# Output projection of an encoder layer: the matmuls that sum the squares a tick and a half later, residual adds on another engine, another order of free banks

## The chip, the cores and the metric

One core of a Trainium2 chip runs the whole program. The metric is device time in microseconds, the median of several runs. The engines are TensorE (PE for matmuls, PEld for its weight loads), VectorE (DVE), ScalarE (ACT), GpSimd (POOL) and SyncE (SP, which here issues DMAs in the order of its queue). Each engine works through its own list of instructions in order, and waits at an instruction until what it needs is there.

## What is computed

A bidirectional encoder layer on two requests (256 and 1024 tokens, width 1024): a half-step SwiGLU network, a mixture of two kinds of attention, a projection of their joint output, a second SwiGLU network, a final norm. The part that matters here, with `oa` and `ob` the two attention outputs, 512 wide each:

```
def rmsnorm(x, g):
    return x * rsqrt(mean(x * x) + EPS) * g
...
mix = concat([rmsnorm(oa, out_norm_a), rmsnorm(ob, out_norm_b)]) @ w_out   # 1024 x 1024
x = x + rmsnorm(mix, mix_post)
x = x + 0.5 * rmsnorm(swiglu(rmsnorm(x, ffn2_pre), ffn2_w_gu, ffn2_w_down), ffn2_post)
```

Everything is fp32; a matmul splits each operand into a high and a low fp32r part and adds three products.

## The kernel before

The class `MixOut` is the output projection. The 1280 tokens are cut into five pieces of 256 and each piece into its two halves of 512 inputs (A and B): ten *operands*, n = 0 to 9, in the order `seq`. An operand has two row tiles of 128 tokens, and each tile two halves of 512 outputs; so `product(n, i, s)` runs four times per operand, each time a group of 12 matmuls (four blocks of inputs, three products) into one bank of PSUM, `yps`. The norms' factors are applied behind the matmul, since they belong to a token. A piece's A half is evacuated by ACT (L1115) into a tile y; its B half is added onto y by DVE (L1124).

`operands` prepares an operand in three stages (the `yield`s part them):

1. SP loads it (`ml`, L1072).
2. ACT makes the high part `mh` (L1077, four instructions) and squares all of it into `sq` (L1078); POOL folds the four blocks of `sq` into one (L1080, two adds); DVE makes the low part in place (L1082, four). There is one buffer `sq`, and L1082 overwrites what L1078 reads.
3. PE sums the squares over the inputs with a matmul against ones (`ssq`, L1088, two of 128x1); DVE adds EPS (L1090); POOL takes the power −1/2 (L1091): the factor `ro`, which the evacuations need.

`done` finishes a tile: SP loads the residual x1 (L1121) and DVE evacuates; ACT squares y (L154) and POOL works out its factor `rs` (L162, L163); DVE multiplies (L1128); POOL adds onto the residual (L1130); SP stores it (L1132); ACT, POOL and DVE do the same for the next norm (L154, L162, L163, L148); SP stores the result (L1136, `xnd`). The second network fetches it again (L1451), POOL forms differences of it (L204 to L216 in `GateUp.blocks`), PE transposes (L197, `tr`), ACT and DVE split (L199, L200).

What sets the order: a pipe (`Pipe`). It counts ticks, one per tile of an operand; a work item comes with a plan of (lag in ticks, place within the tick, cost) for each stage. Stages of a tick run in the order of the place, and the four product groups of the two ticks are laid between them. From the program so written a scheduler makes each engine's list by its own estimate of times, so a moved stage shifts others too. PREP is the plan of `operands`, DONE that of `done`:

```
PREP = [(0, 0, 0.0), (1, 2, 0.0), (3, 0, 0.0)]
DONE = [(0, 1, 0.0), (0, 3, 0.0), (1, 4, 0.0), (2, 2.5, 0.0), (2, 6, 0.0), (3, 6, 0.0), (3, 6, 0.0)]
```

PSUM banks are given out in turn from lists (`Banks.use`): the projection has banks 2 to 5 for products and 6, 7, 0, 1 for transposes and sums of squares; the second network's gate and up products have 0 to 3, and its first transposes take 4 to 7. The last two groups of the projection stand in banks 4 and 5.

Of the kernel before, what the change touches and what calls it, by code (L numbers as in the profile page):

```python
# [13 lines left out]
ALU = mybir.AluOpType  # L14
# [128 lines left out]
def normed(c, x, gain, junk):  # L143

    nc = c.nc
    r = row_factor(c, [square(c, x, junk)])
    yield
    nc.vector.scalar_tensor_tensor(x, x, r, gain, op0=ALU.mult, op1=ALU.mult)  # L148


def square(c, x, junk):

    ss = c.small.tile([128, 1], F32, name="ss")
    c.nc.scalar.activation(junk[:, :x.shape[1]], x, AF.Square, scale=1 / 32, accum_out=ss)  # L154
    return ss


def row_factor(c, sums):

    nc = c.nc  # L160
    r = c.small.tile([128, 1], F32, name="rs")
    nc.gpsimd.tensor_scalar(r, sums[0], sums[1] if len(sums) == 2 else 0.0, EPS, op0=ALU.add, op1=ALU.add)  # L162
    nc.gpsimd.tensor_tensor(r, r, c.mhalf, op=ALU.pow)  # L163
    return r


class GateUp:
# [64 lines left out]
    def prep(self, f):  # L232

        c, nc = self.c, self.c.nc
        g, u = self.raw.pop(f)
        g0, g1, u0, u1 = g[:, 0:4], g[:, 4:8], u[:, 0:4], u[:, 4:8]
        A = self.A[f] = [None] * 7

        def put(i, src):
            A[i] = [self.wp.tile([128, 4, 128], F32R, name=n, bufs=8) for n in ("ah", "al")]  # L240
            split(c, A[i][0], A[i][1], src)

        def tmp(name):
            return self.wp.tile([128, 4, 128], F32, name=name, tag="s", bufs=2)

        put(0, g0)
        yield
        s1, s2 = tmp("s1"), tmp("s2")
        nc.vector.tensor_tensor(s1, u0, u1, op=ALU.add)
        nc.vector.tensor_tensor(s2, s1, g0, op=ALU.subtract)  # L250
        put(1, s2)
        yield
        put(2, g1)
        nc.vector.tensor_tensor(s2, g1, s2, op=ALU.subtract)
        put(4, s1)
        yield
        s3 = tmp("s3")
        nc.vector.tensor_tensor(s3, g0, u0, op=ALU.subtract)
        put(3, s3)
        yield  # L260
        put(5, u1)
        yield
        put(6, s2)
        yield
# [734 lines left out]
class MixOut:  # L999
# [55 lines left out]

    def prep(self, n):
        if n < len(self.seq):
            self.c.pipe.start(self.operands(*self.seq[n], n not in (3, 6)), self.PREP)

    def operands(self, t, half, own):  # L1060

# [47 lines left out]
    def done(self, t, half, i, pss):  # L1109
        c, nc = self.c, self.c.nc  # L1110
        r = self.r[t, half][:, i:i + 1]
        if half == 0:
            y = self.y[t + i] = self.a.tile([128, D], F32, name="y", bufs=4)
            for s, ps in enumerate(pss):
                nc.scalar.activation(y[:, s * 512:(s + 1) * 512], ps, AF.Copy, scale=r)  # L1115
            return
        t += i
        y = self.y.pop(t)
        k = self.k
        x1 = k.tile([128, D], F32, name="x1", bufs=3)  # L1120
        nc.sync.dma_start(x1, self.x1d[t])  # L1121
        for s, ps in enumerate(pss):
            o = y[:, s * 512:(s + 1) * 512]
            nc.vector.scalar_tensor_tensor(o, ps, r, o, op0=ALU.mult, op1=ALU.add)  # L1124
        yield
        junk = k.tile([128, D], BF16, name="junk")
        r = row_factor(c, [square(c, y, junk)])
        nc.vector.scalar_tensor_tensor(y, y, r, self.gmp, op0=ALU.mult, op1=ALU.mult)  # L1128
        yield
        nc.gpsimd.tensor_tensor(x1, x1, y, op=ALU.add)  # L1130
        yield
        nc.sync.dma_start(self.x2d[t], x1)  # L1132
        junk = k.tile([128, D], BF16, name="junk")
        yield from normed(c, x1, self.gf2, junk)
        yield
        nc.sync.dma_start(self.xnd[t], x1)  # L1136
# [25 lines left out]
def encoder(tc, i, out_p, out_s):  # L1162
    nc = tc.nc
    c = Ctx()
# [37 lines left out]
    GATE = {f"{n}{b}": (4 * i + b,) for i, n in enumerate("AB") for b in range(4)}  # L1202
# [275 lines left out]
    mo.close()  # L1478
    gu.open_chunk(1, L.open("xbB", 1))
    gu.work = L.open("gw2", 2)  # L1480
    c.ps.use(**dict(GATE, tr=(4, 5, 6, 7)))
    first = gu.steps(0)
    rest = (None for p in range(2, 5) for _ in gu.blocks(p, *fetch2(p)))
    for step in first[:7]:
# [63 lines left out]
def build(nc, arrays):  # L1548
    ins = {}
    for name, a in arrays.items():  # L1550
        ins[name] = nc.dram_tensor(f"in_{name}_dram", a.shape, mybir.dt.from_np(a.dtype), kind="ExternalInput").ap()
    outs = [nc.dram_tensor(f"out_{i}_dram", s, F32, kind="ExternalOutput").ap()
            for i, s in enumerate(((1, 256, 1024), (1, 1024, 1024)))]
    with tile.TileContext(nc) as tc:  # L1554
        encoder(tc, ins, *outs)
# [12 lines left out]
```

## Time and profile before

| | us |
|---|---|
| median of three runs | 2361.4 (2359.25, 2361.4, 2364.24) |
| profiled execution, whole | 2363.55 |
| its span, first to last instruction | 2361.8 |
| granted TensorE clock, mean | 0.979 |
| output projection, its part behind the attention | about 1376 to 1507 in the span |
| second network behind it | about 1507 to the end |

In the profile's rows, a line number names a line of the kernel, `out<-in` the tiles, `xcount` how many instructions stand in a row, and a bracket at the end how long the engine was idle before it and what released it. A row of a timeline starts with its start and its duration in us. A row of a table of groups has, behind the bar, the busy time in us and the mean in ns of one, and then the idle time ahead of them.

### The profile page before, as it was taken

How to read it: one execution, taken by the hardware profiler on the slowest of the kernel's cores; microseconds unless marked ns; L12 is line 12 of the kernel's file. 1: busy time of each engine (PE TensorE's matmuls, PEld its weight loads, DVE VectorE, ACT ScalarE, POOL GpSimd, SP SyncE). 2: the span in 40 equal slices, each digit the busy share in tenths (PEclk: the TensorE clock that was granted, in tenths of full speed). 3: DMA queues.
4: the chain of work that ended last, by engine and by line, in shares of the span. 5: the costliest groups of instructions: out<-in, count | busy, mean ns of one | idle time of the engine just before them, and what ended most of it. 6: DMA issues, size and time to landing. Idle time of an engine off the chain costs nothing. (4 is left out here: it accounts for less than half of the span.)

```text
span 2361.8 us, 37120 instructions
## 1 busy us (share of the span) xinstructions
PE 2247.5 (95%) x13208; PEld 2047.1 (87%) x13208; DVE 1464.3 (62%) x2575; ACT 980.7 (42%) x2043; POOL 726.7 (31%) x835
## 2 busy tenths in 40 slices
PE   6999999999999999999999788799999999999997
PEld 5999999999788788888888667699999999988876
DVE  7666665655445762996655666666666566544585
ACT  5322322223434543886655643432222222243454
POOL 5222333233000123774332445622122333210012
PEclk9999999999999999999999889899999999999999
DMA  4466666555656653222343544434545655565674
GB/s 137 122 175 188 173 190 174 148 157 145 204 192 200 209 181 108 56 61 57 70 93 79 158 136 167 154 119 137 178 143 170 182 144 155 148 200 186 193 233 155
DMA packets 401418, 358.75 MB, mean 152 GB/s; under 512 B 60433, under 2 KB 326801, under 8 KB 401233
## 3 DMA queue, kind: packets, MB, share of 16 engines
q1 hardware_dynamic: 279280, 287.81, 40.6%
q10 hardware_dynamic: 121952, 68.57, 9.9%
q8 instruction: 104, 1.70, 0.3%
q14 instruction: 82, 0.66, 0.1%
HBM read 237.26 MB, written 111.28 MB: 148 GB/s over the span
## 5 line engine op out<-in xcount | busy, mean ns | idle before, releaser
L280 PE MATMUL gups<-xh,ah 128*128 128x256 f32 (+1 forms) x2464 | 763.3, 310 | 8.1 <-DVE v L289 4.4
L280 PE MATMUL gups<-xh,al 128*128 128x256 f32 (+1 forms) x2464 | 761.5, 309 | 0.0
L280 PE MATMUL gups<-xl,ah 128*128 128x256 f32 (+1 forms) x2464 | 761.1, 309 | 0.0
L463 PE MATMUL dps<-wd,hh 128*128 128x512 f32 x1540 | 480.8, 394 | 4.9 <-ACT hh L69 4.9
L280 PEld LDWEIGHTS gups<-xh,ah 128*128 128x128 f32 x2464 | 466.0, 189 | 12.2 <-DVE v L289 6.5
L280 PEld LDWEIGHTS gups<-xl,ah 128*128 128x128 f32 x2464 | 466.6, 189 | 0.0
L280 PEld LDWEIGHTS gups<-xh,al 128*128 128x128 f32 x2464 | 466.4, 189 | 0.0
L463 PEld LDWEIGHTS dps<-wd,hh 128*128 128x128 f32 x1540 | 290.5, 189 | 67.0 <-ACT hh L69 6.5
L463 PE MATMUL dps<-wd,hl 128*128 128x512 f32 x770 | 304.6, 396 | 6.5 <-DVE hl L72 6.4
L69 ACT ACTIVATE ah<-s 128x512 fp32r<-128x512 f32 x176 | 111.4, 633 | 224.5 <-PE gups L280 170.3
L69 ACT ACTIVATE hh<-hl 128x768 fp32r<-128x768 f32 (+1 forms) x140 | 110.6, 791 | 220.7 <-DMA hl<-hd0s 58.5
L72 DVE TENSOR_TENSOR al<-s,ah 128x512 fp32r<-128x512 f32 x176 | 141.9, 806 | 93.8 <-ACT ah L69 93.1
L72 DVE TENSOR_TENSOR hl<-hl,hh 128x768 fp32r<-128x768 f32 (+1 forms) x140 | 124.6, 891 | 106.3 <-ACT hh L69 104.5
L463 PEld LDWEIGHTS dps<-wd,hl 128*128 128x128 f32 x770 | 145.7, 189 | 44.7 <-DVE hl L72 12.8
L641 POOL TENSOR_TENSOR sb<-sb,rc 128x384 f32<-128x384 f32 (+1 forms) x160 | 123.7, 794 | 171.4 <-DVE rc L639 125.7
L618 PE MATMUL pj<-xh,mh 128*128 128x512 f32 (+1 forms) x432 | 160.5, 372 | 0.9 <-ACT mh L69 0.4
L618 PE MATMUL pj<-xh,ml 128*128 128x512 f32 (+1 forms) x432 | 155.3, 359 | 0.8 <-POOL ml L72 0.5
L618 PE MATMUL pj<-xl,mh 128*128 128x512 f32 (+1 forms) x432 | 154.5, 358 | 0.0
L69 ACT ACTIVATE ah<-raw 128x512 fp32r<-128x512 f32 x132 | 83.5, 633 | 152.3 <-PE gups L280 145.2
L306 ACT ACTIVATE u<-u 128x256 f32<-128x256 f32 x88 | 41.5, 472 | 250.4 <-DVE u L289 222.4
L162 POOL TENSOR_SCALAR rs<-ssq 128x1 f32<-128x1 f32 x20 | 11.5, 575 | 392.9 <-ACT junk L480 392.9
L72 DVE TENSOR_TENSOR wd<-rawd,wd 128x512 fp32r<-128x512 f32 x154 | 105.3, 688 | 42.0 <-ACT wd L69 41.3
(185 smaller groups left out, 3669.8 us busy)
## 6 DMA issues: line engine op xcount, KB each, us to landing
raw<-in_ffn_w_gu_dram SPq DMA_DIRECT2D x88, 512.0 KB, 4.1
rawd<-in_ffn_w_down_dram SPq DMA_DIRECT2D x66, 256.0 KB, 3.4
bx<-in_ffn_w_down_dram SPq DMA_DIRECT2D x22, 512.0 KB, 6.9
bt<-in_ffn_w_down_dram SPq DMA_DIRECT2D x44, 256.0 KB, 5.3
rawd<-td0T SPq DMA_DIRECT2D x44, 256.0 KB, 3.2
rawd<-td1T SPq DMA_DIRECT2D x44, 256.0 KB, 3.3
hl<-hd0s SPq DMA_DIRECT2D x20, 384.0 KB, 3.7
hl<-hd1s SPq DMA_DIRECT2D x20, 384.0 KB, 3.6
```

What stands on the lines that cost most here:

```text
L69: nc.scalar.activation(hi, src, AF.Copy)
L72: (lo_eng or nc.vector).tensor_tensor(lo, src, hi.bitcast(F32), op=ALU.subtract)
L162: nc.gpsimd.tensor_scalar(r, sums[0], sums[1] if len(sums) == 2 else 0.0, EPS, op0=ALU.add, op1=ALU.add)
L280: nc.tensor.matmul(ps, w[:, k, :], x[:, k, :], start=new and k == 0 and m == 0, stop=k == 3 and m == 2, skip_group_check=not new)
L306: self.last_act = nc.scalar.activation(X["u"], X["u"], AF.Silu)
L463: nc.tensor.matmul(ps, a[:, k, :], b, start=i == 0 and v == 0, stop=i == HF - 1 and v == 2)
L618: state["mm"] = nc.tensor.matmul(ps[:, :n], w[:, kk, :], xs[th][:, kk, :], start=first, stop=last)
L641: nc.gpsimd.tensor_tensor(s, s, rc[:, i:i + 1].to_broadcast(list(s.shape)), op=ALU.mult)
```

## The change

Three edits. The third stage of `operands` (the squares' matmuls, L1088, with L1090 and L1091) is put to the end of the tick one later, for operands from 4 on; for the first four it stays where it was. The residual add L1130 goes from POOL to DVE. The first transposes of the second network take banks 6 and 7 before 4 and 5.

```
     def prep(self, n):
         if n < len(self.seq):
-            self.c.pipe.start(self.operands(*self.seq[n], n not in (3, 6)), self.PREP)
+            self.c.pipe.start(self.operands(*self.seq[n], n not in (3, 6)), self.PREP[:2] + [(3, 0, 0.0) if n < 4 else (4, 8, 0.0)])
...
-        nc.gpsimd.tensor_tensor(x1, x1, y, op=ALU.add)
+        nc.vector.tensor_tensor(x1, x1, y, op=ALU.add)
...
-    c.ps.use(**dict(GATE, tr=(4, 5, 6, 7)))
+    c.ps.use(**dict(GATE, tr=(6, 7, 4, 5)))
```

On PE, at operand 4's squares (the first that move; a row stands for one matmul, or xN for N of them, and `woh`, `wol` are the high and low parts of the projection's weights):

```order
 L1103 MATMUL yps<-wol_14862,mh 128x512
 L1103 MATMUL yps<-woh_14861,ml 128x512
-L1088 MATMUL ssq<-ones,sq 128x1 x2
 L1103 MATMUL yps<-woh_14839,mh 128x512
 L1103 MATMUL yps<-wol_14840,mh 128x512
```

They go from here to 36 matmuls later, where operand 5's stood; those of 5 go 48 later, and so on.

On PE, around the ninth operand's third group, four products into which operand 9's squares stood (`tr` are transposes of the second network):

```order
 L1103 MATMUL yps<-wol_14983,mh 128x512
 L1103 MATMUL yps<-woh_14982,ml 128x512
-L197 MATMUL tr<-ident,t_15983 128x128 x4
-L197 MATMUL tr<-ident,t_15984 128x128 x4
+L1088 MATMUL ssq<-ones,sq 128x1 x2
+L197 MATMUL tr<-ident,t_15978 128x128 x4
+L197 MATMUL tr<-ident,t_15979 128x128 x4
 L1103 MATMUL yps<-woh_14897,mh 128x512
 L1103 MATMUL yps<-wol_14898,mh 128x512
 L1103 MATMUL yps<-woh_14897,ml 128x512
 L1103 MATMUL yps<-woh_14901,mh 128x512
-L1088 MATMUL ssq<-ones,sq 128x1 x2
```

The pair that is added is operand 8's, the pair taken out operand 9's. Operand 9's now stands behind two groups of its own operand:

```order
 L1103 MATMUL yps<-wol_14983,mh 128x512
 L1103 MATMUL yps<-woh_14982,ml 128x512
-L197 MATMUL tr<-ident,t_16103 128x128 x4
+L1088 MATMUL ssq<-ones,sq 128x1 x2
+L197 MATMUL tr<-ident,t_16097 128x128 x4
 L197 MATMUL tr<-ident,x 128x128 x4
 L1103 MATMUL yps<-woh_14897,mh 128x512
```

So only operand 9's last two groups follow its squares.

In SP's queue, at the load of operand 8 (`oBd_204`, its row in memory; `x2d`, `xnd` stores of finished tiles, `x1d` loads of residuals):

```order
+L1136 DMA xnd_87<-x_15576 128x1024
+L1136 DMA xnd_88<-x_15642 128x1024
 L1072 DMA ml<-oBd_204 128x4x256
-L1136 DMA xnd_88<-x_15648 128x1024
-L1121 DMA x_16050<-x1d_71 128x1024
-L1132 DMA x2d_79<-x_15799 128x1024
+L1121 DMA x_15846<-x1d_70 128x1024
+L1121 DMA x_16031<-x1d_71 128x1024
```

The load now has the store of tile 88 ahead of it. At the load of operand 9:

```order
-L1121 DMA x_16113<-x1d_72 128x1024
 L1072 DMA ml<-oBd_204 128x4x256
+L1121 DMA x_16107<-x1d_72 128x1024
 L1121 DMA x_16182<-x1d_73 128x1024
 L1451 DMA x<-xnd_88 128x1024
```

It passes one load of a residual.

On DVE, the end of the projection's tail beside the second network's first products (L289), before:

```order
L200 TENSOR_TENSOR xl_15953<-tr,xh_15952 128x4x128
L1124 SCALAR_TENSOR_TENSOR y<-yps,ro,y 128x512
L1128 SCALAR_TENSOR_TENSOR y<-y,rs,ga 128x1024
L148 SCALAR_TENSOR_TENSOR x_16182<-x_16182,rs,gb 128x1024
L289 TENSOR_TENSOR u<-u,gups 128x256
L289 TENSOR_TENSOR v<-u,gups 128x256
L148 SCALAR_TENSOR_TENSOR x_16246<-x_16246,rs,gb 128x1024
```

and now:

```order
L1124 SCALAR_TENSOR_TENSOR y<-yps,ro,y 128x512
L1130 TENSOR_TENSOR x_16182<-x_16182,y 128x1024
L148 SCALAR_TENSOR_TENSOR x_16107<-x_16107,rs,gb 128x1024
L1128 SCALAR_TENSOR_TENSOR y<-y,rs,ga 128x1024
L289 TENSOR_TENSOR u<-u,gups 128x256
L1130 TENSOR_TENSOR x_16246<-x_16246,y 128x1024
L148 SCALAR_TENSOR_TENSOR x_16182<-x_16182,rs,gb 128x1024
L289 TENSOR_TENSOR v<-u,gups 128x256
```

The adds of the last tiles stand between the second network's products.

## The prediction

> **What bounds the kernel now.** I read the page's busy times first, then its 40 slices, then the waits of TensorE, then the stretches of time around the last dip of its clock line, and then the timeline of each engine there.
>
> ```profile
> PE 2247.5 (95%) x13208; PEld 2047.1 (87%) x13208; DVE 1464.3 (62%) x2575; ACT 980.7 (42%) x2043; POOL 726.7 (31%) x835
> ```
>
> TensorE (PE) is busy for 2247.5 of 2361.8 us. So an edit pays only where PE stands idle or runs at a low clock, and the other engines matter where PE waits for them. The waits of PE from 1376 to 1550 us, the output projection and the start of the second FFN:
>
> ```profile
> PE ssq L1088 <- POOL sq L1080: 19.0, 2, 14.0
> PE tr L197 <- DVE y L1124: 4.1, 1, 4.1
> PE gups L280 <- DVE v L289: 1.5, 2, 1.2
> ```
>
> Columns are total, count and longest, in us. The three rows are the stalls of this stage that the change can reach: 24.6 us. The stretches around them (length; busy time of PE, weight loads, DVE, ACT, POOL; granted clock; DMA share):
>
> ```profile
> 1469.70:1483.69 13.99, 0.00 (x1) 0.00 (x1) 6.86 (x7) 4.65 (x9) 3.08 (x3) 0.61 0.54 189
> 1483.69:1508.50 24.81, 24.81 (x124) 21.25 (x125) 18.50 (x24) 9.91 (x18) 18.75 (x18) 0.88 0.37 134
> 1508.50:1530.10 21.60, 14.30 (x103) 13.47 (x101) 15.11 (x16) 7.64 (x14) 17.02 (x14) 0.92 0.45 169
> 1550.00:1600.00 50.00, 50.00 (x338) 49.80 (x337) 29.88 (x52) 14.61 (x29) 10.54 (x8) 1.00 0.42 135
> ```
>
> During the 14 us stall PE does nothing; behind it, it is busy but slower (clock 0.88, then 0.92); after 1550 it is full (50.00 of 50), so what the projection gives back should reach the end.
>
> PE at the two squares' waits and at the banks' wait:
>
> ```profile
> 1409.55 1.01 PE L1088 MATMUL ssq<-ones,sq 128*128 128x1 f32 x4 [4.97 <-POOL sq L1080]
> 1410.42 0.77 PE L1103 MATMUL yps<-woh,mh 128*128 128x512 f32 x1
> 1414.78 0.39 PE L1103 MATMUL yps<-wol,mh 128*128 128x512 f32 x1
> 1415.01 0.40 PE L1103 MATMUL yps<-woh,ml 128*128 128x512 f32 x1
> ```
> ```profile
> 1483.69 1.01 PE L1088 MATMUL ssq<-ones,sq 128*128 128x1 f32 x4 [13.99 <-POOL sq L1080]
> 1484.56 0.77 PE L1103 MATMUL yps<-wol,mh 128*128 128x512 f32 x1
> 1492.57 0.60 PE L197 MATMUL tr<-ident,t 128*128 128x128 f32 x4
> 1493.36 0.48 PE L1103 MATMUL yps<-woh,mh 128*128 128x512 f32 x1
> ```
> ```profile
> 1513.19 0.67 PE L197 MATMUL tr<-ident,x 128*128 128x128 f32 x4 [4.07 <-DVE y L1124]
> 1513.60 0.48 PE L280 MATMUL gups<-xh,ah 128*128 128x256 f32 x1
> 1516.23 1.47 PE L197 MATMUL tr<-ident,t 128*128 128x128 f32 x8
> 1517.66 0.28 PE L280 MATMUL gups<-xl,ah 128*128 128x256 f32 x1
> 1517.78 0.28 PE L280 MATMUL gups<-xh,al 128*128 128x256 f32 x1
> ```
>
> At speed, matmuls of yps start 0.23 us apart (1414.78 to 1415.01) and those of gups 0.12 (1517.66 to 1517.78). After the 4.97 wait ten yps starts take 1410.42 to 1414.78, 4.36 us in place of 2.3; after the 4.07 wait twelve gups take 1513.60 to 1516.23, 2.63 in place of 1.44. So each long stall costs a further 1 to 3 us of low clock.
>
> Why the second wait is 14 us is seen on the other engines (start, duration, engine):
>
> ```profile
> 1443.00 0.47 SPq L1072 DMA_DIRECT2D ml<-oBd  x1
> 1444.74 0.32 SPq L1136 DMA_DIRECT2D xnd<-x  x1
> ```
> ```profile
> 1464.14 8.02 SPq L1136 DMA_DIRECT2D xnd<-x  x2
> 1472.73 0.73 SPq L1072 DMA_DIRECT2D ml<-oBd  x1
> ```
> ```profile
> 1460.63 2.40 POOL L1130 TENSOR_TENSOR x<-x,y 128x1024 f32<-128x1024 f32 x1
> 1462.99 2.27 POOL L204 TENSOR_TENSOR t<-x 128x512 f32<-128x512 f32 x1
> 1468.94 0.56 POOL L163 TENSOR_TENSOR rs<-rs,mhalf 128x1 f32<-128x1 f32 x1
> ```
> ```profile
> 1469.54 2.27 DVE L148 SCALAR_TENSOR_TENSOR x<-x,rs,gb 128x1024 f32<-128x1024 f32 x1 [5.36 <-POOL rs L163]
> 1481.46 3.25 DVE L1082 SCALAR_TENSOR_TENSOR ml<-ml,gon,mh 128x256 fp32r<-128x256 f32 x4 [7.13 <-ACT sq L1078]
> ```
> ```profile
> 1478.78 1.70 ACT L1077 ACTIVATE mh<-ml,gon 128x256 fp32r<-128x256 f32 x4 [11.86 <-DMA ml<-oBd]
> ```
>
> POOL works through the add L1130 and L204 to L208 before it reaches rs at 1468.94; L148 waits for rs; SP's queue stands at the second xnd store for L148, and the load of operand 9 behind it issues only at 1472.73. Its data release ACT at 1478.78, DVE's split at 1481.46, and the squares (ssq(9)) at 1483.69. So the wait at L1088 stands in front of a late load, which the product of operand 9 itself needs.
>
> **The change part by part.**
>
> *Squares later, ssq(4).* It moves past 36 matmuls, so the 4.97 us go, and the slow starts: 4.36 − 10 × 0.23 = 2.1. The two matmuls still run, later. Gain 7.1. Cover: the 36 matmuls are 36 × 0.23 = 8.3 us long, more than the wait, and all their inputs are there, as they ran without a wait before.
>
> *Squares later, ssq(9).* Behind the wait stands work that was ready: 8 matmuls, 8 transposes, 12 matmuls, 8 transposes, up to operand 9's first matmul at 1493.36. It took 1484.56 to 1493.36, 8.8 us at the low clock; at speed 20 × 0.23 + about 1.5 for the transposes (x4 at 1492.57 took 0.4) = 6.1. These 6.1 move under the wait; then PE waits for the split of operand 9 itself. Gain 6.1, with low clock as before. Checked from the other side: were the load no earlier, the split's first quarter would end at 1481.46 + 3.25/4 = 1482.3, 11.1 ahead of 1493.36, less the 2.7 (8.8 − 6.1) of low clock behind it = 8.4 for the two squares together. To reach 7.1 + 6.1 − 2.8 (next term) = 10.4 the load must issue 2.0 us earlier; POOL's add of 2.40, ahead of the rs that the store waits for, leaves that queue.
>
> SP's queue changes at two places. Operand 9's load passes one x1 load (0.4 us, no more: the two stores stay ahead). Operand 8's load, at 1443.00 ahead of a store issued at 1444.74, now comes behind that store, so 1.7 + 0.3 = 2.0 us later in the old times, and later still if its L148 is late. I cost that at nothing: operand 8's data are needed 48 matmuls (11 us) before operand 9's, and what PE then waits at operand 8 comes out of the 7.9 us (13.99 − 6.1) which it would stand at operand 9.
>
> *What the later squares hold up.* There is one sq buffer, so the squares L1078 of operand n wait for ssq(n−1), and the split L1082 waits for L1078. For n from 5 on, two groups (24 × 0.23 = 5.5 us) are left between ssq(n−1) and the first product of n. ACT's square, DVE's split and their neighbours, grouped from 1376 to 1530 us (count, total and mean ns, idle time ahead), and one pair of instructions:
>
> ```profile
> L1082 DVE SCALAR_TENSOR_TENSOR ml<-ml,gon,mh 128x256 fp32r<-128x256 f32 x28 | 23.7, 906 | 12.9 <-ACT sq L1078 12.9
> L1078 ACT ACTIVATE sq<-ml 128x1024 f32<-128x1024 f32 x7 | 7.3, 1049 | 3.9 <-PE ssq L1088 3.8
> L148 DVE SCALAR_TENSOR_TENSOR x<-x,rs,gb 128x1024 f32<-128x1024 f32 x10 | 26.5, 2653 | 11.2 <-POOL rs L163 11.0
> L1128 DVE SCALAR_TENSOR_TENSOR y<-y,rs,ga 128x1024 f32<-128x1024 f32 x10 | 12.8, 1284 | 12.0 <-POOL rs L163 11.9
> L1130 POOL TENSOR_TENSOR x<-x,y 128x1024 f32<-128x1024 f32 x10 | 23.9, 2391 | 4.2 <-DVE y L1128 4.2
> ```
> ```profile
> 1517.95 2.41 POOL L1130 TENSOR_TENSOR x<-x,y 128x1024 f32<-128x1024 f32 x1
> ```
> ```profile
> 1518.03 3.42 DVE L148 SCALAR_TENSOR_TENSOR x<-x,rs,gb 128x1024 f32<-128x1024 f32 x1 [0.76 <-POOL rs L163]
> 1523.57 1.28 DVE L148 SCALAR_TENSOR_TENSOR x<-x,rs,gb 128x1024 f32<-128x1024 f32 x1 [1.27 <-POOL rs L163]
> ```
>
> 1.05 + 0.91 = 2.0 us fit; one L148 (up to 3.4) and one L1128 (1.28) queued ahead of the split make it 6.7, 1.2 too long. The first two groups' banks also stay full until ro is there, after L1090 and POOL's L1091. Bounds: 0, and 1.2 at each of five operands = 6.0. I take two overruns of some 1.4 (operands 6 and 7, where most of the tail's work queues on DVE): −2.8.
>
> *Adds on DVE.* No row shows a 128x1024 tensor add on DVE; the nearest is L1128, the same size with two SBUF inputs, 1.28 us. Ten adds: 12.8 us onto DVE, 23.9 off POOL. In the pair L148 takes 3.42 beside POOL's add and 1.28 alone, so up to 26.5 − 12.8 = 13.7 us of DVE's time were standing still and go. DVE: +12.8 − 13.7, about zero, and the chain of the last tile (add, square, rs, L148) is shorter by 2.4 − 1.3 = 1.1. PE sees nothing of it but through the load above, so no term of its own. Bounds on PE: a gain of the two L289 waits, 1.5; a loss of 4 × 1.28 = 5.1, if each of the last four adds is held for its own length by POOL work that stays (L204 at 2.27 is long enough). I take zero, nearest to L1128: ten of them average 1.284 us in the middle of the same POOL work. The Trainium skill, "SBUF — State Buffer", section "Who interferes with whom", says that a DVE instruction with two SBUF inputs and a GpSimd instruction that reads SBUF exclude one another for the whole instruction; the pair above agrees (3.42 against 1.28). By that rule the moved adds would meet POOL's L204 to L208, and the time would go towards the second rival's.
>
> *Free banks first.* The transposes at 1513.19 waited for the evacuation L1124 of the last product's bank. Banks 6 and 7 carry transposes and squares in the projection, not products. The 4.07 us go, and 2.63 − 1.44 = 1.2 of slow starts: 5.2. Bounds: 0, if the next late thing (DVE's tail, whose L289 products PE needs) stands at the same time; 5.2 + 1.5. I take 5.2, since PE's next waits for DVE are 0.3 and 1.2.
>
> Sum: 7.1 + 6.1 − 2.8 + 5.2 = 15.6 us, of the profiled execution's 2363.55 (span 2361.8). That execution stands 2.15 over the median 2361.4; taken from the median: 2345.8.
>
> **The rivals.**
>
> *The load stays late and the tail binds.* If SP's queue still holds operand 9's load to 1472.7 and DVE's tail takes the bank gain, only the 8.4 remain: 2353.0. For it: the stores and the POOL work L204 to L208 ahead of rs are still there. Against: the add is off POOL.
>
> *The adds are held on DVE.* Each of the last four collides: 15.6 − 5.1 = 10.5, 2350.9. For it: POOL is busy 17.02 of the last 21.6 us; against: some of that is L1130 itself.
>
> *All stalls go.* 7.1 + 13.99 + 2.7 + 5.2 + 1.5 = 30.5: 2330.9. This needs operand 9's load 13.99 − 6.1 = 7.9 us earlier against PE's own time, and PE reaches it 7.1 earlier too; nothing in the change moves SP's queue by so much.
>
> *The one sq buffer becomes the bound (slower).* Square, sums, split and ro of each operand from 5 to 9 follow ssq of the one before; with two L148 beside POOL (6.8 us) and a wait for one rs (0.56) ahead of the split the chain is 2.0 + 6.8 + 0.6 = 9.4 us against 5.5 of room: 3.9 us of stall and 1.2 of low clock (the least seen above), five times, 25.5 us. It takes the place of the 2.8: 15.6 + 2.8 − 25.5 = −7.1, so 2368.5. It decides from a chain of 5.5 + 18.4 / 5 = 9.2 us. For it: L148 takes 2.65 on average now, so most are held. Against: they are held beside L1130, which leaves POOL.
>
> *Nothing is left of it.* The second FFN is paced by its weights and swallows the gain: 2361.4. Against: PE is busy 50.00 of 50 us there, at DMA share 0.42.
>
> **How the numbers follow.** Forecast (gains 11 to 21 us) 0.45, adds held 0.12, late load 0.18, all stalls 0.10, nothing 0.08, the sq buffer 0.07. Faster: 0.45 + 0.12 + 0.18 + 0.10 = 0.85; same 0.08; slower 0.07. A measurement of this kernel tells 0.2%, 4.7 us, from no change (the three runs lie within 5 us). The range runs from 2335.0, part of the way to the case of all stalls, to 2356.5, beyond the late load with its 2.8 of waits counted again (2355.8): the cases outside hold about 0.2.
>
> **What the changed profile would show.** The squares' wait at L1088 gone, and in its place one wait of yps for DVE's ml or ACT's mh, 5 to 8 us in sum, at operands 8 and 9. The wait for L1124 at the transposes gone. L1130 on DVE at about 1.3 us; L148 mostly at 1.3 and not 3.4. New yps waits for ml below 2 us each at operands 6 and 7. I would be wrong if those waits sum to over 6 us, if L1130 on DVE averages above 2 us, or if PE waits 10 us or more for the data of operands 8 and 9.

## The result: 13.9 us faster, and the profile after

| | before | changed |
|---|---|---|
| median, us | 2362.82 (4 runs; 2361.4 for the three shown above) | 2348.93 (4 runs, 2347.86 to 2349.55) |
| ratio | | 0.9946, 95% interval 0.9935 to 0.9957 |
| span of the profiled execution, us | 2361.8 | 2347.4 |
| granted TensorE clock, mean | 0.979 | 0.985 |

The waits of PE from 1376 to 1540 us of the changed kernel (total, count, longest):

```profile
PE yps L1103 <- ACT y L1115: 5.6, 2, 4.3
PE yps L1103 <- DVE ml L1082: 5.1, 2, 4.5
PE tr L197 <- DVE xl L200: 4.7, 1, 4.7
PE tr L197 <- POOL t L204: 2.9, 1, 2.9
PE gups L280 <- DVE v L289: 1.7, 1, 1.7
```

The two waits at the squares (19.0 us) and the one for the banks (4.1) are gone. New are those of products for ACT's evacuation L1115 and of transposes for DVE's split L200. Operand 9's data are not waited for at all: of the two waits for the split L1082, the 4.5 us stand at operand 3, ahead of everything below (3.9 before), and the rest, 0.67, at operand 7.

To see where the time went, three places of PE's list are followed: S, the squares of operand 3, the last that do not move; P, the last product of the projection; T, the transposes that wait for POOL's L204 in the second network. Before:

```profile
1401.19 0.50 PE L1088 MATMUL ssq<-ones,sq 128*128 128x1 f32 x4
...
1506.85 0.40 PE L1103 MATMUL yps<-woh,ml 128*128 128x512 f32 x1
...
1541.20 1.11 PE L197 MATMUL tr<-ident,t 128*128 128x128 f32 x4 [3.01 <-POOL t L204]
```

After:

```profile
1403.07 0.50 PE L1088 MATMUL ssq<-ones,sq 128*128 128x1 f32 x4
...
1500.36 0.40 PE L1103 MATMUL yps<-woh,ml 128*128 128x512 f32 x1
...
1526.91 1.11 PE L197 MATMUL tr<-ident,t 128*128 128x128 f32 x4 [2.87 <-POOL t L204]
```

From S to P it took 105.7 us before and takes 97.3 now (−8.4); from P to T, 34.4 and 26.6 (−7.8). Together −16.2; the work ahead of S took 1.9 more in this execution. 1.5 of these were there before the first L1130 runs (the squares of operand 2 stand at 1377.20 and at 1378.74), and S stands anywhere from 1399 to 1407 in the 14 profiles of this study. The adds do touch this part: the wait at operand 3 is 4.5 us where its neighbour, the first L1130, is on DVE, 3.9 where it is on POOL, and 3.0 without adds (e7 below). From T to the end it is 820.6 and 820.5 us: nothing is given back later.

Within S to P, at the places that both lists have, the changed kernel stands against the old one, S being zero:

| place on PE | before | changed | difference |
|---|---|---|---|
| 48 products after S (then operand 5's squares, now 4's) | 19.5 | 11.8 | −7.7 |
| 192 products after S | 53.9 | 49.0 | −4.9 |
| ahead of operand 9's first product | 91.4 | 76.3 | −15.1 |
| last product (P) | 105.7 | 97.3 | −8.4 |

These lines show the two places where part of the gain goes again:

```profile
1433.73 0.50 PE L1103 MATMUL yps<-woh,mh 128*128 128x512 f32 x1 [1.38 <-ACT y L1115]
...
1462.43 0.79 PE L1103 MATMUL yps<-woh,mh 128*128 128x512 f32 x1 [4.27 <-ACT y L1115]
1463.02 0.63 PE L1103 MATMUL yps<-wol,mh 128*128 128x512 f32 x1
...
1492.36 1.12 PE L197 MATMUL tr<-ident,x 128*128 128x128 f32 x4 [4.74 <-DVE xl L200]
```

At 1462.43 (operand 8's first product) PE waits 4.27 us and then runs at the low clock (0.63 us each); at 1492.36 4.74 us more. The split L200 that it waits for there stands on DVE behind the end of another tile's work:

```profile
1488.17 2.28 DVE L1128 SCALAR_TENSOR_TENSOR y<-y,rs,ga 128x1024 f32<-128x1024 f32 x1 [0.77 <-POOL rs L163]
1490.48 1.23 DVE L1130 TENSOR_TENSOR x<-x,y 128x1024 f32<-128x1024 f32 x1
1491.62 1.28 DVE L200 TENSOR_TENSOR xl<-tr,xh 128x512 fp32r<-128x512 f32 x2
```

### The profile page after: what moved, and what is told of

Its sections match the earlier page's. It is cut to its first block, busy times and chain, and to the rows that moved or that the text cites. A ratio compares the mean times of both kernels' runs of the same rounds, so it can differ in the third digit from the quotient of the medians.

```text
span 2347.4 us, 37114 instructions
## 1 busy us (share of the span) xinstructions
PE 2242.4 (96%) x13208; PEld 2040.6 (87%) x13208; DVE 1457.1 (62%) x2585; ACT 981.3 (42%) x2043; POOL 709.4 (30%) x825
## 5 line engine op out<-in xcount | busy, mean ns | idle before, releaser
L72 DVE TENSOR_TENSOR wd<-rawd,wd 128x512 fp32r<-128x512 f32 x154 | 105.4, 688 | 43.5 <-ACT wd L69 42.4
```

Source lines behind the costliest of these rows:

```text
L72: (lo_eng or nc.vector).tensor_tensor(lo, src, hi.bitcast(F32), op=ALU.subtract)
```

## The experiments

Each ratio is that of 5 to 12 timed runs to runs of the kernel before taken beside them (4 for the changed kernel). "S to P" and "P to T" are read as above off each one's profile, which is a single execution.

| run | ratio to before, 95% | S to P | P to T |
|---|---|---|---|
| before | 1 | 105.7 | 34.4 |
| changed | 0.9946 (0.9935 to 0.9957) | 97.3 | 26.6 |
| e1 squares alone | 0.9981 (0.9973 to 0.9990) | 97.5 | 37.0 |
| e2 adds alone | 0.9965 (0.9953 to 0.9978) | 98.3 | 31.7 |
| e3 banks alone | 0.9997 (0.9988 to 1.0005) | 105.7 | 34.0 |
| e4 squares and banks | 0.9980 (0.9971 to 0.9990) | 95.2 | 36.8 |
| e5 squares and adds | 0.9944 (0.9932 to 0.9956) | 97.1 | 26.6 |
| e6 only operands 4 and 9 later | 0.9955 (0.9942 to 0.9968) | 98.5 | 26.4 |
| e7 adds left out | 0.9949 (0.9937 to 0.9961) | 97.5 | 27.5 |
| e8 before, load of 9 on ACT | 0.9975 (0.9962 to 0.9988) | 97.9 | 35.3 |
| e9 buffers 3, 7 | 0.9939 (0.9923 to 0.9955) | 97.3 | 26.7 |
| e10 loads of 8 and 9 on ACT | 0.9935 (0.9920 to 0.9950) | 92.8 | 26.6 |
| e11 only the last adds on DVE | 0.9960 (0.9948 to 0.9972) | 100.3 | 26.5 |
| e12 load of 8 on ACT | 0.9942 (0.9928 to 0.9956) | 94.6 | 26.6 |

In all but e3 the gain of these two stages in the profile is 1 to 5 us larger than the timed one; the profiles are used for where, the ratios for how much.

### The three edits apart

Squares alone, e1:

```
-            self.c.pipe.start(self.operands(*self.seq[n], n not in (3, 6)), self.PREP)
+            self.c.pipe.start(self.operands(*self.seq[n], n not in (3, 6)), self.PREP[:2] + [(3, 0, 0.0) if n < 4 else (4, 8, 0.0)])
```

> The first edit alone, on the kernel before (adds on POOL, banks as before). Theory S (the later squares carry the gain): the 4.97 us wait at operand 4 goes with its low clock (7.7 us in the traces), later squares cost about 2.8 between operand 5 and 7, and of the 14 us at operand 9 some 6 to 10 come back; 11 to 15 us faster than before, about 2349. Theory L (the adds carried operand 9's share, by freeing POOL and so SP's queue): with the adds on POOL the load of operand 9 stays late, PE waits at operand 9's data, and only 5 to 8 us are gained, about 2356.

Measured: 2357.48, 0.19% or 4.5 us faster by the ratio. S to P gains all of its 8.2 us; P to T loses 2.6. So L is near in the time, but not by its reason: the load of operand 9 was early (1466.19, 63.6 us behind S, against 71.5 before). The loss is behind it. PE in e1, at the second network's first transposes:

```profile
1506.65 1.12 PE L197 MATMUL tr<-ident,x 128*128 128x128 f32 x4 [4.69 <-DVE y L1124]
...
1510.77 1.11 PE L197 MATMUL tr<-ident,x 128*128 128x128 f32 x4 [3.01 <-DVE y L1124]
```

and DVE and POOL there:

```profile
1503.66 2.27 DVE L1128 SCALAR_TENSOR_TENSOR y<-y,rs,ga 128x1024 f32<-128x1024 f32 x1 [3.32 <-POOL rs L163]
...
1507.71 2.34 DVE L148 SCALAR_TENSOR_TENSOR x<-x,rs,gb 128x1024 f32<-128x1024 f32 x1
...
1514.99 3.40 DVE L148 SCALAR_TENSOR_TENSOR x<-x,rs,gb 128x1024 f32<-128x1024 f32 x1 [0.76 <-POOL rs L163]
```
```profile
1501.39 1.28 POOL L204 TENSOR_TENSOR t<-x 128x512 f32<-128x512 f32 x1 [3.69 <-DMA x<-xnd]
...
1503.06 0.56 POOL L163 TENSOR_TENSOR rs<-rs,mhalf 128x1 f32<-128x1 f32 x1
...
1506.62 2.35 POOL L1130 TENSOR_TENSOR x<-x,y 128x1024 f32<-128x1024 f32 x1
```

POOL stands 3.69 us at L204 for a fetch, the factor rs is behind it, DVE's L1128 waits for rs, and the evacuations that free the banks are behind L1128 and the held L148. PE comes earlier and waits there.

Adds alone, e2:

```
-        nc.gpsimd.tensor_tensor(x1, x1, y, op=ALU.add)
+        nc.vector.tensor_tensor(x1, x1, y, op=ALU.add)
```

> The second edit alone (L1130 on DVE). Theory S: the squares still wait; L148 shrinks from 2.65 to about 1.7 us, the load of operand 9 issues 2 to 4 us earlier, so the 14 us wait shrinks by that: 1 to 4 us faster. Theory L: the load issues 5 us or more earlier, 5 to 8 us faster. Theory H (moved adds are held beside POOL's work and hold up the splits): L1130 averages above 1.9 us and the time is 0 to 5 us longer.

Measured: 2353.7, 0.35%, 8.3 us faster, the largest of the three. The load of operand 9 issues 6.3 us earlier (65.2 behind S), which is L's number; the squares' wait at operand 9 falls from 13.99 to 10.72, at operand 4 from 4.97 to 2.90. P to T falls by 2.7. By groups (count, busy us, mean ns), L148 shrinks from 2653 ns to:

```profile
L148 DVE SCALAR_TENSOR_TENSOR x<-x,rs,gb 128x1024 f32<-128x1024 f32 x10 | 15.9, 1586 | 6.7 <-POOL rs L163 6.7
L1130 DVE TENSOR_TENSOR x<-x,y 128x1024 f32<-128x1024 f32 x10 | 13.1, 1313 | 0.1
```

Banks alone, e3:

```
-    c.ps.use(**dict(GATE, tr=(4, 5, 6, 7)))
+    c.ps.use(**dict(GATE, tr=(6, 7, 4, 5)))
```

> The third edit alone. Theory S: the 4.07 us wait for L1124 at the second network's transposes goes with its low clock, 5 us faster. Rival D (DVE's tail is the next late thing): PE waits for DVE's L200 or L289 instead, 0 to 2 us faster.

Measured: 2360.38, no difference that can be told (interval 0.9988 to 1.0005). D holds. Two of PE's waits in e3:

```profile
PE tr L197 <- POOL t L204: 4.5, 1, 4.5
PE tr L197 <- DVE xl L200: 3.3, 1, 3.3
```

The 4.07 us wait for L1124 became 3.26 for L200, which stands just ahead of L1124 in DVE's list; these transposes start 110.8 us behind S in place of 112.0, and the wait at T grew from 3.0 to 4.5.

Two of the three together. Squares and banks, e4:

```
-        nc.vector.tensor_tensor(x1, x1, y, op=ALU.add)
+        nc.gpsimd.tensor_tensor(x1, x1, y, op=ALU.add)
```

(against the changed kernel, as in the next one.)

> The change without its adds (L1130 back on POOL). Theory S with a dear tail: in the changed kernel the transposes of the last operand wait 4.7 us for DVE's split L200, which stands behind an L1130 and an L1128; with the adds on POOL this wait shrinks below 2, and the time is 0 to 5 us under the changed kernel's: 2344 to 2349. Theory L: without the adds the load of operand 9 is late again, PE waits over 5 us at it, and the time is 3 to 8 us above the changed kernel's: 2352 to 2357.

Measured: 2356.97, 8 us over the changed kernel by the ratios. L's time, again not by its reason: operand 9 is early and P too (95.2), and all of the loss is P to T, 36.8 against 26.6. Squares and adds, e5:

```
-    c.ps.use(**dict(GATE, tr=(6, 7, 4, 5)))
+    c.ps.use(**dict(GATE, tr=(4, 5, 6, 7)))
```

> The change without its third edit (banks as before). Alone the third edit had moved the time by 0.8 us. Theory T (DVE's tail is the bound at the end of the projection, so a bank that comes free earlier only lets PE arrive at the next wait): 0 to 2 us over the changed kernel, 2349 to 2351. Theory B (with the tail shortened by the adds, the banks bind, and the 5.4 us that the trace gives back at the first transposes are real): 4 to 6 us over it, 2353 to 2355.

Measured: 2348.45 and the same two stages as the changed kernel. T holds: the third edit gives nothing here either. From e2 to e5 the squares give 0.21%, 5 us, on top of the adds, and from e4 to the changed kernel the adds 0.34%, 8 us, on top of the squares. The place of these gains changes with the company: alone, the squares gain 8.2 us from S to P and the adds 7.4; on top of the other, nearly all of either gain lies from P to T (31.7 to 26.6 for the squares, 36.8 to 26.6 for the adds). For the adds e11, below, shows which of them do it; for the squares no run shows the way.

### What the adds give, and where

The adds left out of the changed kernel, e7:

```
-        nc.vector.tensor_tensor(x1, x1, y, op=ALU.add)
```

> The changed kernel with the residual adds L1130 left out altogether (the stored x is then the residual alone; every other step runs). Theory T: ten adds of 1.40 us go from DVE, the last four from the tail that PE waits for; 4 to 7 us under the changed kernel, and the 4.7 us wait of the transposes for DVE's L200 shrinks by 2.4 or more. Rival F (the adds on DVE are free, covered by waits for rs on POOL): within 2 us of the changed kernel.

Measured: 2348.51; without any add the time is that of the changed kernel. F holds, T falls: on DVE the adds are free, as far as the interval of some 3 us to either side can tell. P to T is 27.5: PE waits 3.1 us for DVE's L289 in place of 1.7.

Only the adds of the last four tiles on DVE, e11:

```
+        (nc.vector if 3 < t < 8 else nc.gpsimd).tensor_tensor(x1, x1, y, op=ALU.add)
```

> The changed kernel with only the adds of the last four tiles on DVE, the first six back on POOL. Theory T (what the adds give is the tail behind the last product: 26.3 us from there to the transposes of the second network's third pair, against 34 to 37 with POOL's adds): the tail stays 26 to 28 us, the first six adds matter little, and the time is within 2 us of the changed kernel, 2347 to 2351. Rival E (the gain is spread over all ten adds, through the rs that wait behind them on POOL): about half of the adds' gain of 8 us is lost, 2352 to 2354.

Measured: 2352.16. P to T stays at 26.5, as T says: the last four adds make all of that stage. S to P is 3.0 us longer, so by place the first six give some 3 us as well, and the median is in E's range; the intervals of the two ratios overlap, so the time alone does not tell it. Each theory has one half of it.

### What the later squares and the loads give

Only operands 4 and 9 later, e6:

```
+ [(4, 8, 0.0) if n == 4 or n == 9 else (3, 0, 0.0)]
```

> The changed kernel, but only operands 4 and 9 have their squares later; 5 to 8 go back to lag 3. Theory O (late factors ro cost what the trace shows: 1.4 us at operand 6, 4.3 and low clock at operand 8): these waits go and the time is 3 to 9 us under the changed kernel, 2340 to 2346. Theory T (DVE's tail, with operand 9's load in front of it, is the bound; PE only waits somewhere else): the waits move to operand 9 or the transposes and the time is within 2 us of the changed kernel.

Measured: 2348.84, T. The waits for L1115 are gone, and 10.3 us of waits for L200 stand in their place (two; 4.7 in one in the changed kernel), beside one of 2.4 us at operand 5's squares. Moving 5 to 8 neither gives nor costs anything that the intervals tell.

The old kernel with operand 9's load issued by ACT, e8:

```
+        (nc.scalar if (t, half) == self.seq[9] else nc.sync).dma_start(o, src.rearrange("j p t -> p j t"))
```

> The kernel before, with one edit: the load of operand 9 is issued from ACT's queue in place of SP's, some 7 us earlier (behind L1115 at about 1465.4 instead of 1472.7), past the stores that wait for L148. Theory Q (the 14 us wait at operand 9's squares is the late load behind SP's stores): the wait shrinks to 4 to 8 us and the time is 4 to 8 us under the kernel before. Theory T: the wait shrinks, but DVE's tail ends no earlier, PE waits for it later, and the time gains 0 to 3 us.

Measured: 2354.96, 0.25%, 5.9 us faster. The load issues 62.3 us behind S in place of 71.5; it and the wait at operand 9's squares:

```profile
1463.50 0.39 ACTq L1072 DMA_DIRECT2D ml<-oBd  x1
...
1473.37 1.01 PE L1088 MATMUL ssq<-ones,sq 128*128 128x1 f32 x4 [4.34 <-POOL sq L1080]
```

Q holds: 13.99 became 4.34 by the load's place alone. So 9.7 of the 14 us were the load's place in SP's queue. Three different edits (e1, e2, e8) each bring S to P to 97.5 to 98.3: each takes some 8 us out of this stage, and two of them together don't take it twice (e5, 97.1). In the times the three are worth 4.5, 8.3 and 5.9 us.

What keeps S to P at 97? Operand 9's load again, was the guess. In e9, operand 7 uses the shared buffers in place of operand 6:

```
-            self.c.pipe.start(self.operands(*self.seq[n], n not in (3, 6)), ...
+            self.c.pipe.start(self.operands(*self.seq[n], n not in (3, 7)), ...
```

> The changed kernel with operand 7 in place of operand 6 in the buffers that the second network's fetches also use, so that operand 9's load needs the buffer of operand 6 (free 48 matmuls earlier) and stands ahead of four stores in SP's queue. In the ten profiles so far the projection's last product begins to end 33 to 36 us after that load issues, whatever was changed. Theory Q (that load sets the end of the projection): it issues 6 to 15 us earlier, the last product ends 3 to 8 us earlier against operand 3's squares (97.5 us in the changed kernel), and the time is 2 to 6 us under the changed kernel, 2343 to 2347. Rival P (PE's own work and the waits for DVE set it, and the load only went along): the last product stays within 1.5 us, other waits grow, and the time is within 2 us of the changed kernel, or above it as the fetches of the second network start later.

The load issued at 42.4 us behind S, 21.7 earlier, and S to P stayed at 97.3. Q falls as the limit of the changed kernel; the fetches of the second network came later, and PE waited for POOL's L204 (2.5 us) and for L200. The timed 2346.24 is not told from the changed kernel's. Then the loads of both 8 and 9 on ACT, in the changed kernel, e10:

```
+        (nc.scalar if (t, half) in self.seq[8:] else nc.sync).dma_start(o, src.rearrange("j p t -> p j t"))
```

> The changed kernel with the loads of operands 8 and 9 issued by ACT, past SP's stores. Theory Q: operand 9's load issues at about 62 us after operand 3's squares or earlier (64.1 in the changed kernel), operand 8's some 3 us earlier; the last product ends 1 to 3 us earlier, 2345 to 2348. Rival P: no change of the time beyond 1 us; the wait for L200 or for the factor ro grows by what the load gained.

Here S to P fell by 4.5. The wait for L1115 at operand 8 fell from 4.27 to 2.45 us; the time, 2346.72, is in Q's range, and the interval too wide to tell it from the changed kernel's. Which of the two loads it was, e12 asks (8 alone):

```
+        (nc.scalar if (t, half) == self.seq[8] else nc.sync).dma_start(o, src.rearrange("j p t -> p j t"))
```

> The changed kernel with operand 8's load alone issued by ACT (operand 9's stays in SP's queue behind its stores). Theory V (in the changed kernel operand 8's load, put behind one more store, holds ACT at L1077, behind it operand 7's squares L1078, so the factor ro of operand 7 and the evacuations that operand 8's products wait for): the wait of yps for L1115 shrinks from 4.3 to 2.5 or less, the last product comes 3 to 5 us earlier against operand 3's squares (93 to 94.5 us against 97.5), as with both loads moved, and the time is 2 to 4 us under the changed kernel. Theory Q (it was operand 9's load): the last product stays at 96.5 to 97.5 us and the time within 1 us of the changed kernel.

Measured: S to P 94.6, the wait for L1115 2.44 in place of 4.27; V holds by the place of the gain. Of e10's 4.5 us, 2.7 are operand 8's load; most of the rest is clock and not the other load, since behind the same wait PE ran at a granted clock of 0.51 for 3.1 us here and at 1.00 in e10. The way from the load to the wait is another than V said: operand 7's squares are in time at PE in both kernels, and the delay goes through DVE's list. In the changed kernel:

```profile
1442.77 1.31 ACT L1077 ACTIVATE mh<-ml,gon 128x256 fp32r<-128x256 f32 x3 [6.32 <-DMA ml<-oBd]
1443.99 1.04 ACT L1078 ACTIVATE sq<-ml 128x1024 f32<-128x1024 f32 x1
```
```profile
1445.07 3.28 DVE L1082 SCALAR_TENSOR_TENSOR ml<-ml,gon,mh 128x256 fp32r<-128x256 f32 x4 [2.72 <-ACT sq L1078]
...
1454.38 2.31 DVE L1128 SCALAR_TENSOR_TENSOR y<-y,rs,ga 128x1024 f32<-128x1024 f32 x1 [2.23 <-POOL rs L163]
...
1456.72 2.20 DVE L1130 TENSOR_TENSOR x<-x,y 128x1024 f32<-128x1024 f32 x1
...
1458.84 0.15 DVE L1090 TENSOR_SCALAR ro<-ssq 128x2 f32<-128x2 f32 x1
```
```profile
1460.96 0.70 POOL L1091 TENSOR_TENSOR ro<-ro,mhalf 128x2 f32<-128x2 f32 x1
```

ACT waits for operand 8's load with operand 7's square behind it; DVE's split of 7 waits for that; two tiles' L1128 and L1130 follow in DVE's list, and the factor ro of operand 7 (L1090, L1091) only behind them, 6.8 us after its squares were summed at 1452.06. In e12 the split starts 38.6 us behind S in place of 42.0, L1090 53.0 in place of 55.8:

```profile
1439.93 2.83 DVE L1082 SCALAR_TENSOR_TENSOR ml<-ml,gon,mh 128x256 fp32r<-128x256 f32 x4
...
1454.31 0.15 DVE L1090 TENSOR_SCALAR ro<-ssq 128x2 f32<-128x2 f32 x1
```

The times of e9, e10 and e12 are the lowest of the study (2346.2 to 2346.7), but their intervals hold the changed kernel's ratio: whether one of them beats it is open.

## Why the prediction was right in sum and wrong in its parts

The time, 2348.9, lies 3.1 us over the forecast of 2345.8: a gain of 13.9 by the medians and 12.8 by the ratio, against 15.6. The mechanism of the late load (e8) and of the low clock behind operand 4's wait held. Of the signs that it named, the squares' waits and the one for L1124 are gone, L1130 averages 1.40 us, and new waits at operands 6 and 7 stay below 2; the 5 to 8 us of waiting for the data of operands 8 and 9 did not come. The terms did not hold:

- *Squares, 7.1 + 6.1 − 2.8 = 10.4.* By place: −7.7 for the first, as said (7.1). At operand 9 the sum foresaw PE standing at its data; no such wait came (−15.1 ahead of its first product): the load issued 64.1 us behind S in place of 71.5, and PE had been held at operands 6 to 8 instead (next point). The load needed no help of the adds for that; with the squares alone it issued at 63.6 (e1). In time, the squares are worth 4.5 us alone and 5 on top of the adds: half of the term. The failed part is the reading that what PE wins there reaches the end; 6.7 us of it went again at and behind the wait for L200, which stood behind DVE's tail, and in e1 a further 2.6 went between P and T.
- *Later squares hold up, 2.8.* 1.38, 0.67 and 4.27 us were measured at operands 6, 7 and 8, 6.3 in sum, with low clock behind the last. The term was worked out from the one sq buffer; the two large waits came from the late factor ro in DVE's and POOL's lists, which the prediction named and did not price. e6 shows that they cost nothing in the end that the times tell, since other waits take their place.
- *Operand 8's load behind one more store, 0.* e12 puts 2.7 us of S to P on it; in the times it cannot be told. The step's argument, that it comes out of operand 9's wait, fell with that wait.
- *Adds, 0.* They are worth 8 us alone and 8 on top of the others, the largest part, and the step that failed most: it said that PE sees nothing of them but through the load. The step counted DVE's own time (+12.8 − 13.7) and 1.1 us of the last tile's chain. Two things were missed. First, POOL's list: without 2.4 us per add, rs and so the stores and operand 9's load came 6.3 us earlier (e2); the prediction named this and granted it 2.0. Second, the tail: P to T falls from 36.8 (e4) to 26.5 with the last four adds alone (e11). Each tile of the last operands passes POOL twice for rs, and in e4 some of these passes stand behind an L1130, and one behind an L204 that itself waits for a fetch. The last L148 ends 12.7 us behind P's start in the changed kernel; in e4 it was 22.2.
- *Banks, 5.2.* Alone and with the rest, no difference that can be told (e3, e5). The bound of 0 that the prediction kept was the right end: the next late thing, DVE's L200, stood 1.2 us ahead of L1124.

The tail in e4:

```profile
1497.44 1.26 POOL L204 TENSOR_TENSOR t<-x 128x512 f32<-128x512 f32 x1 [4.22 <-DMA x<-xnd]
...
1510.97 2.40 POOL L1130 TENSOR_TENSOR x<-x,y 128x1024 f32<-128x1024 f32 x1
...
1516.57 1.28 DVE L148 SCALAR_TENSOR_TENSOR x<-x,rs,gb 128x1024 f32<-128x1024 f32 x1 [1.26 <-POOL rs L163]
```

and its end in the changed kernel:

```profile
1511.75 1.28 DVE L148 SCALAR_TENSOR_TENSOR x<-x,rs,gb 128x1024 f32<-128x1024 f32 x1
```

So the sum came near by luck: 5.2 for the banks and 5.4 too much for the squares covered a missing 8 for the adds. Two small slips stand in the working: the chances of the cases outside its range add up to 0.25 and not 0.2, and of the 8.8 us from 1484.56 to 1493.36 only those to about 1490 were at the low clock (the 2.7 us lost there are right). Of the rivals, *the adds are held on DVE* had its mechanism right in part:

```profile
L1128 DVE SCALAR_TENSOR_TENSOR y<-y,rs,ga 128x1024 f32<-128x1024 f32 x10 | 15.9, 1587 | 10.4 <-POOL rs L163 9.9 <-ACT xh L199 0.4
L148 DVE SCALAR_TENSOR_TENSOR x<-x,rs,gb 128x1024 f32<-128x1024 f32 x10 | 14.9, 1486 | 4.4 <-POOL rs L163 4.4
L1130 DVE TENSOR_TENSOR x<-x,y 128x1024 f32<-128x1024 f32 x10 | 14.0, 1402 | 0.1
```

DVE has 44.8 us of these three where L148 and L1128 were 39.3, 5.5 more and not zero: L1130 takes 1.22 alone and 2.20 at 1456.72, beside POOL's L205 and L208, and L1128 is held now as it was not before.

```profile
1455.68 2.15 POOL L205 TENSOR_TENSOR t<-x,t 128x512 f32<-128x512 f32 x1
1457.80 2.24 POOL L208 TENSOR_TENSOR x<-x 128x512 f32<-128x512 f32 x1
```

L205 ends 1.11 us behind the start of that L1130, which then takes 1.09 more, and L208 beside it takes 2.24 where it takes 1.28 alone. That is the Trainium skill's rule of a DVE instruction with two SBUF inputs and a GpSimd instruction that reads SBUF ("SBUF — State Buffer", "Who interferes with whom"), and the trace agrees with it, 2.20 against 1.22. Only its price was nothing that the times tell (e7): the groups above show 9.9 and 4.4 us in which DVE waited for rs in any case.

*The load stays late and the tail binds* has its second half right: the load was early, but DVE's tail took the gain of the banks. *All stalls go* was set aside because nothing would move SP's queue by 7.9 us. With the squares alone the load did move by 7.9 us behind S (e1); what stood against this rival were new waits, 6.3 us at operands 6 to 8 and 4.74 at L200. *The one sq buffer* (slower) did not occur: the longest wait at these operands was 4.27 us, once. *Nothing is left* is refuted by T to the end, 820.6 and 820.5.

## What to carry to other kernels

An instruction that is moved off an engine is worth what stands behind it in that engine's list, not its own time: here adds of 2.4 us on POOL held the factors that stores, loads and evacuations waited for. Before terms are added, ask whether two edits take back the same wait: three edits each took some 8 us out of the same stage, and two of them no more than one, and a wait that went at one bank came back at a neighbour in the same engine's list. And where a transfer is late, read what stands ahead of it in its queue; giving it another queue is a cheap test of that.

## What was not expected of the hardware

A wait of 2.44 us can bring the low clock, and the length of a wait near that does not decide whether it does. In e12, PE:

```profile
1457.80 0.79 PE L1103 MATMUL yps<-woh,mh 128*128 128x512 f32 x1 [2.44 <-ACT y L1115]
1458.39 0.63 PE L1103 MATMUL yps<-wol,mh 128*128 128x512 f32 x1
```

Products then took 0.63 us in place of 0.39 until 1460.9, 3.1 us, at a granted clock of 0.51. At the same product in e10:

```profile
1458.63 0.50 PE L1103 MATMUL yps<-woh,mh 128*128 128x512 f32 x1 [2.45 <-ACT y L1115]
1458.97 0.39 PE L1103 MATMUL yps<-wol,mh 128*128 128x512 f32 x1
```

Here the clock stayed at 1.00, and so it did in e2 behind a wait of 2.90 us (at 1406.50). In e6 the slow products began 1.7 us after a wait of 2.38 us had ended (1417.09 to 1418.82) and lasted 3.4 us. What decides between these cases is not shown. Behind the 1.38 us wait at 1433.73 of the changed kernel the next product took 0.39.
